# Moving GpSimd's large element-wise products in the front of a hybrid attention/SSM/MoE layer to VectorE and ScalarE

## Chip, cores, metric

The kernel runs on one core of a Trainium2 chip. The metric is the device time of one execution in microseconds (us). The kernel before takes 1189.6 us, the median of 3 runs (1189.0 to 1190.3).

## What is computed

One layer of a streaming encoder, batch 1, 256 frames, 1024 features, fp32, with 16 meta tokens put in front (272 rows). The parts that matter here:

```python
h = layer_norm(concat(meta, x), ln_in_g, ln_in_b)
q, k, v, u = split(h @ w_in)                      # 512 columns each
lam = exp(sum(lq1 * lk1)) - exp(sum(lq2 * lk2)) + lam_init
att = diff_attention(q, k, v, lam, ...)           # 4 heads, two softmaxes each, chunk-causal
ssm = s5_ssm(u, a_re, a_im, log_step, b, c, ...)  # complex diagonal recurrence, then GLU
h = layer_norm(2**0.25 * h + concat(att, ssm) @ w_out, ln1_g, ln1_b)
h = layer_norm(2**0.25 * h + moe(h), ln2_g, ln2_b)  # top 4 of 32 experts, each 3 matrices of 1024x1024
```

## The kernel before, in words

The order of the instructions on each engine is the order of the program text (the schedule is written by hand); every engine works through its own queue in order and waits on semaphores where data is needed. All loads are issued on SyncE's queue (SP), also in order.

**Front** (lines 145 to 870). Rows are loaded, normalised (lines 198 to 217), transposed on TensorE into hT (line 237), and projected with w_in: u first (line 389), then q (439), k and v (`proj`, lines 429 to 434). The SSM is done four frames at a time. VectorE works out the step, the decay and the rotations: `exp_poly` (248) for exponentials, and sines and cosines of 8 multiples of the angle (285 to 309). The table ED (line 314, in buffer slot 6) holds the rotors of 68 steps for 16 blocks; it is filled by doubling, seven steps k of six products or sums each (`cmul`, line 262, called on GpSimd at 324), of 16 times 1, 2, 4, ..., 32 and 4 elements per partition. `powers` (361) multiplies the input matrix Bb by the powers RW (on VectorE, line 381) and the output matrix CC by the powers FW (on GpSimd, line 472); each of its two halves ri is two products of 1024 elements and a sum or difference that is written in two partition halves (line 377 or 375) between zeros into AB. TensorE transposes the input side of AB (459) into BAT, which lies in the buffers that held the temporaries of `cmul` and `powers` (xs5, slots 5a and 5b); ScalarE and VectorE take turns with the copies (463, 465). Then GpSimd overwrites AB with the output side.

**Rounds** (623 to 659). For each of four blocks: `states_a` (TensorE, 553), `states_b` (VectorE, 565 to 577: products, a scan, products), `scores_a` (TensorE 588, VectorE 593, ScalarE's exponentials 597), `scores_b` (VectorE, 602 to 607), with a projection of k or v in between whose copy out of PSUM is ScalarE's. PSUM has 8 banks, handed out in turn by `nb` (77). Meanwhile GpSimd does the output side, a memset (477) and the affine step of the input norm on the residual rows hr (478 to 480).

**Output side of the front** (668 to 868). Products for lags within four frames (674, 678, copied by `lag_b`, 687, into ML), `split_w` (535), which splits w_out into a rounded high part and a low part (cast on ScalarE or VectorE, subtraction on GpSimd or VectorE), `av_a` (726; per head a transpose, copies 735 and 736, and the products 749 of the head before), `av_b`, `out_a` to `out_c`, and `mix` (829) with w_out. Then `norm1` (919), `turn1` (931), `affine1` (937, GpSimd) and the router (`route_a` to `route_c`).

**Experts** (1329 on). 384 chunks of 1 MB of expert weights are streamed through a ring of 18 half-slots (line 488) in the slots 0 to 8; a chunk is issued (`chunk`, 500) when the program has reached it and its half-slot is free. The first chunks are issued between the steps of the front, as its buffers come free: slot 6 after the last `states_b`, slot 3 after w_out's first half is split, slot 4 after `out_a`, the others after the mix and the GLU. One loop at line 1238 handles overfull experts late in the run.

Of the kernel before, what the change touches and what calls it, by code (L numbers as in the profile page):

```python
# [11 lines left out]
F32 = mybir.dt.float32  # L12
# [3 lines left out]
AF = mybir.ActivationFunctionType  # L16
OP = mybir.AluOpType
# [4 lines left out]
D = 1024  # L22
# [42 lines left out]
def hybrid_layer(ctx, tc, I, out):  # L65
# [18 lines left out]
    def slot(i, shape, name, dt=F32):  # L84
        return per.tile(shape, dt, name=name, tag=f"slot{i}")
# [23 lines left out]
    def pt(shape, name, dt=F32, tag=None, bufs=None):  # L109
        return pool.tile(shape, dt, name=name, tag=tag or name, bufs=bufs)  # L110
# [16 lines left out]
    def load(dst, name, off, dims):  # L127
        return SP.dma_start(dst, pap(I[name], off, dims))
# [24 lines left out]
    load_win("u", 0, 1536, 2)  # L153
    for j, n in enumerate(("lambda_q1", "lambda_q2", "lambda_k1", "lambda_k2")):
        load(lam4[:, j, :], n, 0, [[0, 128], [1, 64]])
    eb = slot(6, [128, 4096], "eb")
    bt = eb[:, 3264:3776].rearrange("p (r a c) -> p r a c", r=2, a=16)
    for j, n in enumerate(("b_re", "b_im")):
# [103 lines left out]
    def cmul(eng, dr, di, ar_, ai_, br_, bi_, u, v):  # L262
        eng.tensor_tensor(u, ar_, br_, op=OP.mult)
        eng.tensor_tensor(v, ai_, bi_, op=OP.mult)
        eng.tensor_tensor(dr, u, v, op=OP.subtract)
        eng.tensor_tensor(u, ar_, bi_, op=OP.mult)
        eng.tensor_tensor(v, ai_, br_, op=OP.mult)
        eng.tensor_tensor(di, u, v, op=OP.add)
# [6 lines left out]
            V.tensor_scalar(hT[:, db, :], PS[:, hb[db], :NP], VC[:, db:db + 1], VC[:, 8 + db:9 + db],  # L275
                            op0=OP.mult, op1=OP.add)

    step = pt([128, 16], "step")
    exp_poly(step, LS, 16, "e1")
    sm = [pt([128, 16], f"sm{j}") for j in range(10)]  # L280
    ar, mag, den, er, t1, t2, fr, fi, r4, dt = sm
    V.tensor_scalar(ar, A_RE, -1e-4, None, op0=OP.min)
# [37 lines left out]
    ge = [tq[4 + j].rearrange("p (a c) -> p a c", a=16) for j in range(2)]  # L320
    for k in range(7):
        n = min(2 ** k, 68 - 2 ** k)
        c_, s_ = ((a[:, 1 + k, :, None]).to_broadcast([128, 16, n]) for a in (cs, sn))
        cmul(G, ED[:, 0, :, 2 ** k:2 ** k + n], ED[:, 1, :, 2 ** k:2 ** k + n],
             ED[:, 0, :, 0:n], ED[:, 1, :, 0:n], c_, s_, ge[0][:, :, :n], ge[1][:, :, :n])


    FW = pt([128, 2, 4, 16], "FW")
# [29 lines left out]

    cmul(V, Bb[:, 0], Bb[:, 1], bc16(fr), bc16(fi), bt[:, 0], bt[:, 1], bu, bv)

    def powers(eng, dst, src, tab, sgn, ta, tb):
# [6 lines left out]
        for ri, (j0, j1) in enumerate(((0, 1), (1, 0))):  # L368
            op = sgn[ri]
            eng.tensor_tensor(ta, sv(0), tv(j0), op=OP.mult)  # L370
            eng.tensor_tensor(tb, sv(1), tv(j1), op=OP.mult)
            for g2 in range(2):
                h = slice(64 * g2, 64 * g2 + 64)
                if op == "r":
                    eng.tensor_tensor(dst[h, ri, :, :, g2], tb[h], ta[h], op=OP.subtract)
                else:
                    eng.tensor_tensor(dst[h, ri, :, :, g2], ta[h], tb[h],
                                      op=OP.add if op == "+" else OP.subtract)

    tmp = xs5[0].rearrange("p (r a t c) -> p r a t c", r=2, a=16, t=4)  # L380
    powers(V, AB, Bb, RW, "-+", tmp[:, 0], tmp[:, 1])


    while bank[0] % 4:
# [57 lines left out]
    lt = et([128, 2, 64], "lt")  # L442
    xl, el = et([128, 2], "xl"), et([128, 2], "el")
    V.tensor_tensor(lt, lam4[:, 0:2], lam4[:, 2:4], op=OP.mult)
    V.tensor_reduce(xl, lt, axis=AX.X, op=OP.add)
    exp_poly(el, xl, 2, "e3")
    lam = pt([128, 1], "lam")
    V.tensor_sub(lam, el[:, 0:1], el[:, 1:2])
    V.tensor_scalar(lam, lam, LAM_INIT, None, op0=OP.add)
# [15 lines left out]
                S.activation(BAT[ri][:, 4 * a:4 * a + 4], srcv, AF.Copy)  # L465


    sl0, bc = (slot(f"0{c}", [128, 2, D], "sl0") for c in "ab")
    load(bc[:, 0, :], "ln_in_g", 0, [[0, 128], [1, D]])
    load(bc[:, 1, :], "ln_in_b", 0, [[0, 128], [1, D]])  # L470
    tmc = [sl0[:, j].rearrange("p (a t c) -> p a t c", a=16, t=4) for j in range(2)]
    powers(G, AB, CC, FW, "+r", tmc[0], tmc[1])
    MG = slot(1, [128, 2, 2048], "MG")
    load(MG[:, 1, :], "w_glu", 0, [[512, 128], [128 * 512, 4], [1, 512]])
    ML = MG[:, 0, :].rearrange("p (f q c) -> p f q c", f=4, q=4)
    WG = MG[:, 1, :].rearrange("p (k f) -> p k f", k=4)
# [249 lines left out]
    def av_a(i, between=None):  # L726
        blks = ((0, 128), (1, 16)) if i == 0 else ((0, 128), (1, 128), (2, 16))
        nf = len(blks) - 1
        wts = []
        for h in range(4):  # L730
            tb = nb()
            for blk, n in blks:
                T.transpose(PS[:n, tb, blk * 128:blk * 128 + 128], PW[h, i][:, blk * 128:blk * 128 + n], ident)
            wT = lt_([128, 3, 128], "wT", bufs=2)
            S.activation(wT[:, :nf], PS[:, tb, :nf * 128].rearrange("p (a q) -> p a q", a=nf), AF.Copy)
            V.tensor_copy(wT[:16, nf], PS[:16, tb, nf * 128:nf * 128 + 128])
            wts.append(wT)
# [193 lines left out]
    def turn1(i):
        TB[i] = nb(2)
# [539 lines left out]
```

## Time and profile before

| | |
|---|---|
| median of 3 runs | 1189.6 us |
| the profiled execution's own time | 1188.67 us |
| its span in the profile | 1186.9 us |
| TensorE (PE) busy | 1038.4 us, 87% |
| VectorE (DVE) busy | 360.6 us, 30% |
| ScalarE (ACT) busy | 127.2 us, 11% |
| GpSimd (POOL) busy | 169.6 us, 14% |
| read from HBM | 423.5 MB, 358 GB/s over the span |
| mean granted TensorE clock | 0.952 of full speed |

PE, PEld, DVE, ACT, POOL and SP are TensorE's matmuls and weight loads, VectorE, ScalarE, GpSimd and SyncE. Times in rows are microseconds from the start of the span. L12 is line 12 of the kernel. In `out<-in`, names are the program's tile names; where tiles share memory a row can show another tile's name (xs for the temporaries, sl and s8b for scratch).

### The profile page before, as it was taken

The page shows a single profiled execution, that of the slowest core. Times are in us where ns is not written, and L with a number is a line of the kernel's source. Part 1 is how long each engine was busy: PE and PEld are TensorE (multiplying, and loading weights), DVE is VectorE, ACT ScalarE, POOL GpSimd, SP SyncE. Part 2 cuts the span into 40 slices and gives each one's busy share as a digit, 9 for nine tenths or more (in the row PEclk, how much of TensorE's full clock was granted, in tenths as well). Part 3 has the DMA queues.
Part 4 walks back from the last instruction along what each step waited for, and adds up shares of the span by engine and source line. Part 5 has one row for each costly group of instructions (what it writes and reads, how often), then busy time and mean ns, then how long its engine had stood idle before and what let it go on. Part 6 is the DMA issues. An engine that isn't in the chain of part 4 may idle for free. (4 is left out here: it accounts for less than half of the span.)

```text
span 1186.9 us, 16400 instructions
## 1 busy us (share of the span) xinstructions
PE 1038.4 (87%) x6572; PEld 529.2 (45%) x6572; DVE 360.6 (30%) x737; ACT 127.2 (11%) x286; POOL 169.6 (14%) x259
## 2 busy tenths in 40 slices
PE   6858798989999988999999987899999999998195
PEld 5646686343543443445434433343443344343042
DVE  7999656222212110221122121121122112121113
ACT  1411442100100000001000000000000000000010
POOL 2990414200200110002001011001101010010001
PEclk9978797989999998999999998999999999999699
DMA  7702478789999999999999999999999897999994
GB/s 214 259 0 76 158 270 332 309 324 423 420 421 421 421 420 421 421 420 420 421 421 421 419 421 421 421 421 421 421 412 404 356 403 274 396 365 422 385 372 196
DMA packets 72314, 425.67 MB, mean 359 GB/s; under 512 B 14925, under 2 KB 15546, under 8 KB 23210
## 3 DMA queue, kind: packets, MB, share of 16 engines
q1 hardware_dynamic: 72234, 424.58, 88.5%
q8 instruction: 53, 0.87, 0.3%
q14 instruction: 27, 0.22, 0.1%
HBM read 423.50 MB, written 1.87 MB: 358 GB/s over the span
## 5 line engine op out<-in xcount | busy, mean ns | idle before, releaser
L1156 PE MATMUL PS<-wx,xgp 128*32 128x256 f32 (+2 forms) x3008 | 464.2, 476 | 14.7 <-DMA wx<-in_w_up 8.6
L1156 PEld LDWEIGHTS PS<-wx,xgp 128*32 128x32 f32 (+2 forms) x3008 | 186.5, 130 | 272.8 <-issue 207.8
L1156 PE MATMUL PS<-wx,yT 128*32 128x256 f32 (+2 forms) x1504 | 231.0, 473 | 21.7 <-DVE yT L1189 17.6
L1156 PEld LDWEIGHTS PS<-wx,yT 128*32 128x32 f32 (+2 forms) x1504 | 92.2, 129 | 148.2 <-issue 95.8
L914 POOL COPY si<-P 96x32 bf16<-96x32 bf16 (+2 forms) x32 | 7.4, 234 | 789.3 <-PE PS L1150 759.8
L1178 DVE TENSOR_SCALAR PS<-PS 128x256 f32<-128x256 f32 (+2 forms) x33 | 22.6, 683 | 191.0 <-PE PS L1156 191.0
L1203 DVE COPY yc<-PS 32x256 f32<-32x256 f32 (+1 forms) x39 | 20.1, 514 | 169.0 <-ACT yc L1205 169.0
L1211 PE MATMUL PS<-yc,gt 128*128 128x512 f32 x120 | 58.6, 620 | 13.6 <-DVE yc L1203 5.7
L1212 DVE TENSOR_TENSOR acc<-PS,acc 128x512 f32<-128x512 f32 x60 | 41.4, 691 | 92.9 <-PE PS L1211 92.7
L1150 PE MATMUL PS<-B,si 96*32 96x256 bf16 (+2 forms) x282 | 39.9, 333 | 32.8 <-SPq L1238 25.9
L1118 PEld LDWEIGHTS PS<-ohp,hr 128*128 128x128 f32 x512 | 63.5, 200 | 8.4 <-issue 8.4
L1118 PE MATMUL PS<-ohp,hr 128*128 128x128 f32 x512 | 65.8, 288 | 0.2 <-DVE ohp L1110 0.2
L1172 DVE TENSOR_SCALAR g<-PS 128x256 f32<-128x256 f32 (+1 forms) x27 | 14.9, 553 | 152.5 <-PE PS L1156 122.1
L1205 ACT ACTIVATE yc<-PS 32x256 f32<-32x256 f32 (+1 forms) x39 | 17.4, 446 | 244.2 <-PE PS L1156 237.8
L1211 PEld LDWEIGHTS PS<-yc,gt 128*128 128x128 f32 x120 | 18.7, 188 | 51.6 <-DVE acc L1212 19.8
L1150 PEld LDWEIGHTS <-si 96*32 96x32 bf16 (+2 forms) x282 | 11.8, 100 | 60.0 <-issue 55.2
L1189 DVE COPY yT<-PS 128x512 f32<-128x512 f32 (+1 forms) x39 | 22.5, 590 | 45.2 <-PE PS L1188 45.2
L1173 ACT ACTIVATE PS<-g 128x256 f32<-128x256 f32 (+1 forms) x27 | 13.2, 491 | 206.3 <-DVE g L1172 206.3
L1108 POOL TENSOR_SCALAR gop<-io,PMs,Gs 128x32 f32<-128x32 f32 (+2 forms) x60 | 33.3, 569 | 0.0
L1172 DVE TENSOR_SCALAR yc<-PS 128x1024 f32<-128x1024 f32 x6 | 7.4, 1225 | 78.3 <-PE PS L1156 78.3
L1122 ACT ACTIVATE xgp<-PS 128x512 f32<-128x512 f32 x16 | 9.6, 597 | 192.5 <-PE PS L1118 192.5
L1110 POOL TENSOR_SCALAR ohp<-io,PMs 128x32 f32<-128x32 f32 (+2 forms) x60 | 24.9, 433 | 0.0
(380 smaller groups left out, 847.9 us busy)
## 6 DMA issues: line engine op xcount, KB each, us to landing
wx<-in_w_gate SPq DMA_DIRECT2D x128, 1024.0 KB, 19.7
wx<-in_w_up SPq DMA_DIRECT2D x128, 1024.0 KB, 19.8
wx<-in_w_down SPq DMA_DIRECT2D x127, 1024.0 KB, 19.7
w_u<-in_w_in SPq DMA_DIRECT2D x2, 1024.0 KB
w_q<-in_w_in SPq DMA_DIRECT2D x1, 2048.0 KB
w_k<-in_w_in SPq DMA_DIRECT2D x2, 1024.0 KB
w_v<-in_w_in SPq DMA_DIRECT2D x1, 2048.0 KB
wo<-in_w_out SPq DMA_DIRECT2D x2, 1024.0 KB
```

Source lines behind the costliest of these rows:

```text
L1108: eng.tensor_scalar(dst[:, i, o:o + m], iv, pc, gg[:, i, t:t + 1], op0=OP.is_equal, op1=OP.mult)
L1110: eng.tensor_scalar(dst[:, i, o:o + m], iv, pc, None, op0=OP.is_equal)
L1118: T.matmul(PS[:, 4 + h, k * 128:k * 128 + n], hr[:, i, rows_of(db)], oh_[:, i, :n], start=(i == 0), stop=(i == 1))
L1150: T.matmul(o, sel[:, :m], B96[:, w, f * n:f * n + n], start=True, stop=False)
L1156: T.matmul(PS[(f % nf) * m:(f % nf) * m + m, b + f // nf, :n], xT(kb), c[:, f * n:f * n + n], start=False, stop=(kb == 7))
L1172: V.tensor_scalar(g_, r_, 7.0, None, op0=OP.min)
L1178: V.tensor_scalar(r_, r_, 7.0, -7.0, op0=OP.min, op1=OP.max)
L1189: V.tensor_copy(yT[:, 4 * a:4 * a + nk], PS[:, b, :nk * 128].rearrange("p (k s) -> p k s", k=nk))
L1203: V.tensor_copy(d_, s_)
L1205: S.activation(d_, s_, AF.Copy)
L1211: T.matmul(PS[:, b], gt[:n, i * 128:(i + 1) * 128], yc[:n, h * 512:(h + 1) * 512], start=True, stop=True)
L1212: V.tensor_tensor(acc[:, i, h * 512:(h + 1) * 512], PS[:, b], acc[:, i, h * 512:(h + 1) * 512], op=OP.add)
```

## The change

- `load_win("u")` comes after the four lambda loads; lambda's two sums are made before the transposes are evaluated, and its exponentials share one `exp_poly` with the step.
- The first four rotor steps stay on GpSimd; steps 4 to 6 run on VectorE (`rotors`), after the input side's products.
- `powers` becomes `products` (VectorE, three instructions on all partitions, into a temporary) and `between_zeros` (ScalarE, two copies of 64 partitions into AB). On the input side ScalarE's copies stand between those of the queries, on the output side the whole (`output_matrices`) stands between `scores_a` and `scores_b` of rounds 0 and 1.
- The residual's affine step goes from GpSimd to VectorE, in eight pieces, two after each head's copies in `av_a(0)`. Its two vectors get a slot of their own, 9; the scratch for dynamic DMAs is cut to 1024 bytes to make room.
- `split_w` casts on ScalarE and subtracts on VectorE throughout; the second half of w_out is split in one call, later.
- `norm1(1)` is applied on ScalarE, with a small product (n1) on VectorE in front.

```diff
+    lt = et([128, 2, 64], "lt")
+    V.tensor_tensor(lt, lam4[:, 0:2], lam4[:, 2:4], op=OP.mult)
+    V.tensor_reduce(VC[:, 80:82], lt, axis=AX.X, op=OP.add)
     V.tensor_copy(VC[:, 32:80], PS[:, pb, 304:352])
...
-    step = pt([128, 16], "step")
-    exp_poly(step, LS, 16, "e1")
+    steps = pt([128, 18], "step")
+    exp_poly(steps, VC[:, 64:82], 18, "e1")
+    step, el = steps[:, :16], steps[:, 16:18]
...
-    for k in range(7):
+    def rotors(eng, k, ta, tb):
         n = min(2 ** k, 68 - 2 ** k)
-        cmul(G, ED[:, 0, :, 2 ** k:2 ** k + n], ...)
+        src = ED[:, 0:2, :, 0:n]
+        ta, tb = (t_[:, :32 * n].rearrange("p (j a c) -> p j a c", j=2, a=16) for t_ in (ta, tb))
+        for dst, fac in ((ta, cs), (tb, sn)):
+            for j in range(2):
+                eng.tensor_tensor(dst[:, j], src[:, j], fac[:, 1 + k, :, None].to_broadcast([128, 16, n]), op=OP.mult)
+        new = ED[:, :, :, 2 ** k:2 ** k + n]
+        eng.tensor_tensor(new[:, 0], ta[:, 0], tb[:, 1], op=OP.subtract)
+        eng.tensor_tensor(new[:, 1], tb[:, 0], ta[:, 1], op=OP.add)
+
+    for k in range(4):
+        rotors(G, k, tq[4], tq[5])
...
+    def products(ri, src, tab, op, ta, tb):
...
+        V.tensor_tensor(ta, sv(0), tv(ri), op=OP.mult)
+        V.tensor_tensor(tb, sv(1), tv(1 - ri), op=OP.mult)
+        if op == "r":
+            V.tensor_tensor(ta, tb, ta, op=OP.subtract)
+        else:
+            V.tensor_tensor(ta, ta, tb, op=OP.add if op == "+" else OP.subtract)
+
+    def between_zeros(dst, ri, src):
+        for g2 in range(2):
+            h = slice(64 * g2, 64 * g2 + 64)
+            S.activation(dst[h, ri, :, :, g2], src[h], AF.Copy)
+
+    pwf = lw([128, 1024], "pw", tag="vr")
...
-    powers(V, AB, Bb, RW, "-+", tmp[:, 0], tmp[:, 1])
+    for ri in range(2):
+        products(ri, Bb, RW, "-+"[ri], tmp[:, ri], pw)
+    for k in (4, 5, 6):
+        rotors(V, k, pwf, xs5[1][:, 0:1024])
...
     for h in range(4):
         S.activation(qT[:, h, :], proj("q", h, NM), AF.Copy, scale=0.125)
+        if h % 2:
+            between_zeros(AB, h // 2, tmp[:, h // 2])
...
-    powers(G, AB, CC, FW, "+r", tmc[0], tmc[1])
+    def output_matrices(ri):
+        products(ri, CC, FW, "+r"[ri], tmc[ri], pw)
+        between_zeros(AB, ri, tmc[ri])
...
-    for i in range(2):
-        G.tensor_tensor(hr[:, i], hr[:, i], bc[:, 0], op=OP.mult)
-        G.tensor_tensor(hr[:, i], hr[:, i], bc[:, 1], op=OP.add)
+    def residual_rows(n):
+        for _ in range(n):
+            i, h, j = rr_todo.pop(0)
+            hf = hr[:, i, h * 512:(h + 1) * 512]
+            V.tensor_tensor(hf, hf, bc[:, j, h * 512:(h + 1) * 512], op=(OP.mult, OP.add)[j])
...
-        for k, on_act, eng in ks:
-            if on_act:
-                S.activation(W_HI[j][k], W_OUT[j][k], AF.Copy)
-            else:
-                V.tensor_copy(W_HI[j][k], W_OUT[j][k])
-            eng.tensor_sub(W_LO[j][k], W_OUT[j][k], W_HI[j][k].bitcast(F32))
+        for k in ks:
+            S.activation(W_HI[j][k], W_OUT[j][k], AF.Copy)
+        for k in ks:
+            V.tensor_sub(W_LO[j][k], W_OUT[j][k], W_HI[j][k].bitcast(F32))
...
     scores_a(0, 1)
+    output_matrices(0)
...
     scores_a(1, 1)
+    output_matrices(1)
...
     value_rows(1, vt1)
-    split_w(1, 5, 0, ((0, True, G), (1, True, G)))
...
-    split_w(1, 5, 0, ((2, False, G), (3, False, G)))
+    split_w(1, 5, 0, (0, 1, 2, 3))
...
             wts.append(wT)
+            if i == 0:
+                residual_rows(2)
...
-    split_w(0, 8, 2, ((2, True, G), (0, False, V), (1, True, V)))
+    split_w(0, 8, 2, (0, 1))
     out_a(0)
     out_a(1)
-    av_a(1, lambda: split_w(0, 8, 2, ((3, True, G),)))
+    av_a(1, lambda: split_w(0, 8, 2, (2, 3)))
...
+        if i:
+            n1 = wt([128, 1], "n1")
+            V.scalar_tensor_tensor(n1, m1[:, 0:1], -1.0, r1, op0=OP.mult, op1=OP.mult)
         for f in range(2):
             hf = hr[:, i, f * 512:(f + 1) * 512]
-            V.tensor_scalar(hf, hf, m1[:, 0:1], r1, op0=OP.subtract, op1=OP.mult)
+            if i:
+                S.activation(hf, hf, AF.Identity, bias=n1, scale=r1)
+            else:
+                V.tensor_scalar(hf, hf, m1[:, 0:1], r1, op0=OP.subtract, op1=OP.mult)
```

## Rows read from the trace of the kernel before

**Rows 1.** Windows: us, busy time (x instructions) per engine, granted clock, DMA share, GB/s.

```profile
60.00:80.00 20.00, 13.84 (x64) 11.06 (x64) 18.55 (x12) 1.48 (x3) 19.57 (x10) 0.84 0.00 0
100.00:120.00 20.00, 20.00 (x221) 16.27 (x220) 18.79 (x59) 6.30 (x25) 0.00 (x0) 0.99 0.39 135
...
205.00:210.00 5.00, 4.91 (x24) 3.78 (x26) 4.17 (x16) 0.00 (x0) 2.77 (x1) 0.55 0.00 0
...
300.00:350.00 50.00, 49.10 (x351) 24.43 (x344) 8.26 (x14) 3.62 (x7) 8.32 (x18) 1.00 1.01 420
```

The engine columns of rows 1 are PE, PEld, DVE, ACT and POOL.

**Rows 2.** Waits of SyncE's queue, whole span: us in total, times, longest.

```profile
SPq L522 <- PE PS L1156: 257.6, 138, 18.1
```

**Rows 3.** Timeline, 63 to 87 us, VectorE and GpSimd: start us, us, instruction.

```profile
64.65 5.02 POOL L377 TENSOR_TENSOR AB<-sl 64x1024 f32<-64x1024 f32 x2
64.88 2.58 DVE L568 TENSOR_TENSOR s8b<-s8b 128x272 f32<-128x272 f32 x1
...
84.40 2.34 POOL L480 TENSOR_TENSOR hr<-hr,sl 128x1024 f32<-128x1024 f32 x1
84.44 2.31 DVE L603 TENSOR_TENSOR a<-a,lam 128x1 f32<-128x1 f32 x1
```

**Rows 4.** Timeline, 92 to 127 us, VectorE: the undisturbed rounds and their end.

```profile
92.74 0.71 DVE L565 TENSOR_TENSOR s8b<-PS,eb 128x544 f32<-128x544 f32 x1
...
94.48 0.43 DVE L568 TENSOR_TENSOR s8b<-s8b 128x272 f32<-128x272 f32 x1
...
121.77 4.91 DVE L683 COPY m<-ident 32x32 f32<-32x32 f32 x4
```

**Rows 5.** Timeline, 38 to 64 us, up to the first states_b; idle before in brackets.

```profile
38.11 1.47 DVE L370 TENSOR_TENSOR xs<-xs,RW 128x1024 f32<-128x1024 f32 x1
...
59.31 2.47 DVE L463 COPY BAT<-PS 128x512 f32<-128x512 f32 x4
...
60.40 1.08 ACT L465 ACTIVATE BAT<-PS 128x512 f32<-128x512 f32 x2 [7.32 <-POOL eb L268]
...
63.13 0.72 DVE L565 TENSOR_TENSOR s8b<-PS,eb 128x544 f32<-128x544 f32 x1 [1.35 <-PE PS L553]
```

**Rows 6.** Timeline of VectorE, two-input instructions without GpSimd's products beside them.

```profile
165.23 1.22 DVE L845 TENSOR_TENSOR bf<-bf,bp 96x1024 f32<-96x1024 f32 x1
...
204.76 0.68 DVE L939 TENSOR_TENSOR hr<-hr,bc 128x512 f32<-128x512 f32 x1
```

**Rows 7.** Line 540 on ScalarE, whole span: duration in ns, min/median/max.

```profile
L540 ACT ACTIVATE wh<-wo x5: 1039/1049/1062, 120.8 to 148.6; 128x1024 fp32r<-128x1024 f32 x5
```

**Rows 8.** DMA rate, 0 to 60 us in 40 slices of 1.5 us.

```profile
GB/s 0 134 358 294 367 403 400 233 31 27 64 68 180 367 406 395 291 150 15 63 333 403 404 393 390 384 384 88 72 366 116 30 356 395 249 399 352 5 0 0
```

**Rows 9.** Timeline of VectorE, 127 to 134 us: lag copies, first attention weights.

```profile
127.88 3.16 DVE L696 COPY MG<-KS 32x512 f32<-32x512 f32 x8
...
132.98 0.71 DVE L736 COPY wT<-PS 16x128 f32<-16x128 f32 x2 [0.61 <-ACT wT L735]
```

**Rows 10.** Timeline of VectorE, av_a(1), its copy for head 2.

```profile
150.41 0.28 DVE L736 COPY wT<-PS 16x128 f32<-16x128 f32 x1 [1.42 <-ACT wT L735]
```

**Rows 11.** Windows, from out_a(1) to the mix; columns as in rows 1.

```profile
144.60:161.00 16.40, 16.25 (x134) 14.13 (x133) 8.80 (x16) 7.51 (x20) 3.36 (x2) 1.00 0.37 132
```

**Rows 12.** Timelines of GpSimd and VectorE, 193 to 197 us, norm1(1).

```profile
193.86 1.27 POOL L939 TENSOR_TENSOR hr<-hr,bc 128x512 f32<-128x512 f32 x1
...
193.93 2.88 DVE L929 TENSOR_SCALAR hr<-hr,m,r 128x512 f32<-128x512 f32 x2 [0.67 <-POOL r L195]
```

**Rows 13.** Timeline of TensorE, 94 to 110 us: states_a(2) and states_a(3), projections.

```profile
94.14 3.68 PE L553 MATMUL PS<-u,BAT 128*128 128x68 f32 x16 [10.77 <-DVE s8b L566]
97.61 5.19 PE L432 MATMUL PS<-hT,w_k 128*128 128x272 f32 x16
102.64 3.83 PE L432 MATMUL PS<-hT,w_v 128*128 128x272 f32 x16
...
107.69 1.90 PE L553 MATMUL PS<-u,BAT 128*128 128x68 f32 x16
```

More of the change, by code (lines that the diff above doesn't have):

```diff
@@ L152, in hybrid_layer @@
     load(ls[32:48], "log_step", 0, [[2, 16], [1, 2]])
-    load_win("u", 0, 1536, 2)
     for j, n in enumerate(("lambda_q1", "lambda_q2", "lambda_k1", "lambda_k2")):
         load(lam4[:, j, :], n, 0, [[0, 128], [1, 64]])
+    load_win("u", 0, 1536, 2)
     eb = slot(6, [128, 4096], "eb")
@@ L319, in hybrid_layer @@
     tq = [x_[:, 512 * j:512 * j + 512] for x_ in xs5 for j in range(4)]
-    ge = [tq[4 + j].rearrange("p (a c) -> p a c", a=16) for j in range(2)]
-    for k in range(7):
+    def rotors(eng, k, ta, tb):
         n = min(2 ** k, 68 - 2 ** k)
-        c_, s_ = ((a[:, 1 + k, :, None]).to_broadcast([128, 16, n]) for a in (cs, sn))
-        cmul(G, ED[:, 0, :, 2 ** k:2 ** k + n], ED[:, 1, :, 2 ** k:2 ** k + n],
-             ED[:, 0, :, 0:n], ED[:, 1, :, 0:n], c_, s_, ge[0][:, :, :n], ge[1][:, :, :n])
+        src = ED[:, 0:2, :, 0:n]
[8 more added lines that the diff above has]
+        rotors(G, k, tq[4], tq[5])
     FW = pt([128, 2, 4, 16], "FW")
@@ L359, in hybrid_layer @@
     cmul(V, Bb[:, 0], Bb[:, 1], bc16(fr), bc16(fi), bt[:, 0], bt[:, 1], bu, bv)
-    def powers(eng, dst, src, tab, sgn, ta, tb):
+    def products(ri, src, tab, op, ta, tb):
         def sv(j):
@@ L366, in tv @@
             return tab[:, j].rearrange("p t a -> p a t")[:, :, :, None].to_broadcast([128, 16, 4, 16])
[L368 to L375, printed above, removed]
-                else:
-                    eng.tensor_tensor(dst[h, ri, :, :, g2], ta[h], tb[h],
-                                      op=OP.add if op == "+" else OP.subtract)
+        V.tensor_tensor(ta, sv(0), tv(ri), op=OP.mult)
[9 more added lines that the diff above has]
+    pwf = lw([128, 1024], "pw", tag="vr")
+    pw = pwf.rearrange("p (a t c) -> p a t c", a=16, t=4)
     tmp = xs5[0].rearrange("p (r a t c) -> p r a t c", r=2, a=16, t=4)
-    powers(V, AB, Bb, RW, "-+", tmp[:, 0], tmp[:, 1])
+    for ri in range(2):
+        products(ri, Bb, RW, "-+"[ri], tmp[:, ri], pw)
+    for k in (4, 5, 6):
+        rotors(V, k, pwf, xs5[1][:, 0:1024])
     while bank[0] % 4:
@@ L439, in hybrid_layer @@
         S.activation(qT[:, h, :], proj("q", h, NM), AF.Copy, scale=0.125)
[L442 to L446, printed above, removed]
+        if h % 2:
+            between_zeros(AB, h // 2, tmp[:, h // 2])
     lam = pt([128, 1], "lam")
@@ L465, in hybrid_layer @@
                 S.activation(BAT[ri][:, 4 * a:4 * a + 4], srcv, AF.Copy)
-    sl0, bc = (slot(f"0{c}", [128, 2, D], "sl0") for c in "ab")
+    sl0 = slot("0a", [128, 2, D], "sl0")
+    bc = slot(9, [128, 2, D], "bc")
     load(bc[:, 0, :], "ln_in_g", 0, [[0, 128], [1, D]])
@@ L477, in hybrid_layer @@
     G.memset(MG[:, 0, :], 0.0)
-    for i in range(2):
-        G.tensor_tensor(hr[:, i], hr[:, i], bc[:, 0], op=OP.mult)
-        G.tensor_tensor(hr[:, i], hr[:, i], bc[:, 1], op=OP.add)
+    def residual_rows(n):
[3 more added lines that the diff above has]
+            V.tensor_tensor(hf, hf, bc[:, j, h * 512:(h + 1) * 512], op=(OP.mult, OP.add)[j])
+    rr_todo = [(i, h, j) for i in range(2) for h in range(2) for j in range(2)]
     def rows_of(kb):
@@ L537, in split_w @@
             W_HI[j], W_LO[j] = parts4(s_, "wh", FR), parts4(l_, "wl", FR)
-        for k, on_act, eng in ks:
-            if on_act:
-                S.activation(W_HI[j][k], W_OUT[j][k], AF.Copy)
-            else:
-                V.tensor_copy(W_HI[j][k], W_OUT[j][k])
-            eng.tensor_sub(W_LO[j][k], W_OUT[j][k], W_HI[j][k].bitcast(F32))
+        for k in ks:
+            S.activation(W_HI[j][k], W_OUT[j][k], AF.Copy)
+        for k in ks:
+            V.tensor_sub(W_LO[j][k], W_OUT[j][k], W_HI[j][k].bitcast(F32))
     XS, VB = {}, {}
@@ L607, in scores_b @@
         V.scalar_tensor_tensor(w[:, :nk], s_[:, 0, :nk], r_[:, 0:1], s_[:, 1, :nk], op0=OP.mult, op1=OP.subtract)
-    vr = lw([128, 3, 512], "vr")
     def values(h):
@@ L639, in hybrid_layer @@
     states_b(2)
+    vr = lw([128, 3, 512], "vr")
     vt0 = values(0)
@@ L1461 @@
     from concourse.bass_utils import run_bass_kernel_spmd
-    nc = bacc.Bacc("TRN2", target_bir_lowering=False, num_devices=1)
+    nc = bacc.Bacc("TRN2", target_bir_lowering=False, num_devices=1, dynamic_dma_scratch_size=1024)
     arrays = {f"in_{n}": a for n, a in layout(inputs).items()}
```

## The prediction

> **What bounds the kernel now.** I began with the stages (busy time of each engine by stretch) and asked which of them can pass a saving on. From 300 us on the DMA engines are full at 420 GB/s [rows 1], so the weight stream cannot be made faster there; only its start can move. At 205 to 210 us, just before the first expert, they move nothing [rows 1]: the ring of weight buffers is full, and what was loaded before has slack. From there on a load waits until TensorE releases a buffer: of what SyncE's queue waits for, TensorE's expert products are the longest item, 257.6 us in 138 waits [rows 2]. So the moment at which TensorE starts on the experts sets the stream behind it, and a saving in the front should reach the end nearly one for one.
>
> Inside the front, 60 to 80 us stands out: VectorE and GpSimd are both busy all the time, TensorE only 13.84 of 20 us and DMA not at all; at 100 to 120 us, with GpSimd idle, TensorE is full [rows 1]. The timeline of the two vector engines says why. The subtraction of line 568 takes 2.58 us beside GpSimd's line 377 (two instructions, 5.02 us). A 128x1 product, line 603, takes 2.31 us: it starts 0.04 us after GpSimd's line 480 and ends with it, near 86.75 [rows 3]. The same line 568 takes 0.43 us once GpSimd has stopped [rows 4]. VectorE stands still while GpSimd runs a large product.
>
> **The change part by part.** The sum is made along VectorE's order, against the profiled execution's 1188.67 us.
>
> *1. Up to the first round of states.* Before, states_b(0) starts at 63.13, after ScalarE had waited 7.32 us for GpSimd's rotors, whose temporary its copy overwrites [rows 5]. After, VectorE goes on at 38.11 with six full-height products and sums of 1024 elements. The first of these takes 1.47 us with GpSimd beside it [rows 5]; a 1024-wide two-input instruction without GpSimd takes 1.22, a 512-wide one 0.68 [rows 6]. GpSimd still makes the four small rotor steps for the first few microseconds, so I take three at 1.47 and three at 1.22: 8.1 us, to 46.2. The last three rotor steps are six instructions each, of 256, 512 and 64 elements; the line through the two prices of rows 6 gives 0.41, 0.68 and 0.21: 7.8 us, to 54.0. Then lambda (I take 0.4; its sums and polynomial have moved forward) and four copies of BAT, 2.47 [rows 5]: to 56.9. ScalarE's four writes of halves into AB cost about 1.05 each, the price of a 128x1024 copy there [rows 7]; two fall between the copies of queries and two before the key's, where ScalarE otherwise waits for TensorE's projections: nothing. **-6.2 us.** Bounds: all six at 1.22 gives -7.0; all at 1.47, and VectorE held once by ScalarE's copies for 2.1, gives -3.3.
>
> [...]
>
> The four lambda loads now stand ahead of w_u in SyncE's queue and hold its two issues back by their own four, under 2 us. The traffic that w_u ends is over by the ninth slice of 1.5 us, at 12 [rows 8], and TensorE waits for hT until 14: that wait hides about 2 us; if it doesn't, +1. Lambda's two new VectorE instructions come where VectorE waits for TensorE's transposes: nothing.
>
> *2. The four rounds of states and scores.* Before, 63.13 to 121.77 (where line 683 starts): 58.6 us. The three undisturbed rounds took 92.74 to 121.77, 29.0 us, so 9.7 each [rows 4]. After: four such rounds, 38.7, and output_matrices twice, three instructions at 1.22 each: 7.4. Together 46.1, to 103.0: **-12.5 us.** At 1.47 each it is -11.0. Behind output_matrices scores_b is queued, whose exponentials ScalarE makes meanwhile. ScalarE's four writes of halves (1.05 each) hold back its copies of keys 2 and 3, which are wanted a round later: nothing, or 2 us where TensorE's banks run out.
>
> *3. To the first weights of attention.* Before, 121.77 to 132.98, 11.2 us, of which line 683, four 32x32 copies, takes 4.91 beside GpSimd's subtractions [rows 4, 9]. After, I take 0.7 for it, 0.7 for line 685, 0.3 waiting for KS, 3.16 for line 696 [rows 9]; then four casts on ScalarE at 1.05 [rows 7] and four subtractions on VectorE at 1.22, the first beside the second cast: 4.9 and 1.2 in front. To 114.0, 11.0 us: **-0.2** (-1.5 to +1.5). W_OUT's other loads come earlier with everything else.
>
> *4. The residual's affine step,* four instructions of 2.34 on GpSimd [rows 3], is now eight on VectorE of 512 at 0.68, two after each head's copy in av_a(0), which put 1.4 us between that copy and the next. TensorE's and ScalarE's steps for a head run beside them; at the last head I find VectorE 0.7 us behind. **+0.7** (0 to +2).
>
> *5. split_w(0) in av_a(1).* Two casts (2.1) and two subtractions (2.4) now stand between heads 1 and 2, where one cast stood and the subtraction ran on GpSimd. VectorE's copy for head 2, at 150.41 before [rows 10], comes 1.7 us later. From 144.6 to the mix at 161 TensorE is busy 16.25 of 16.40 us [rows 11], so no gap behind it absorbs that: I take **+1.3** (0 to +2).
>
> *6. norm1(1).* VectorE's two instructions of line 929 take 2.88 us, because GpSimd's line 939 started 0.07 us ahead of them [rows 12]. They go to ScalarE, but the small product n1 ahead of them stays on VectorE and meets the same GpSimd instruction, as line 603 did [rows 3, 12]: it ends near 195.2. ScalarE would then end near 196.5, where VectorE ended at 196.81, but the router's copy of rows 0 is queued behind it on ScalarE, and TensorE's transposes behind the product that wants that copy. **+1.4** (-0.5, if n1 finds a gap, to +1.6).
>
> Sum: -6.2 - 12.5 - 0.2 + 0.7 + 1.3 + 1.4 = -15.5, 1173.2 us for the profiled execution. The median of the runs, 1189.6, lies 0.9 above it: **1174.0**, rounded.
>
> **The rivals.**
> - *The late terms cost nothing* (4 to 6 lie beside other work): -18.9, 1170.7. For it: two of them stand where TensorE waits as well. Against: TensorE full behind term 5 [rows 11]. 0.16.
> - *ScalarE's copies hold VectorE.* If a second product waits until ScalarE has read the first one's half of a temporary, some 2.1 us come back at two or three places: about 1179. Against: the halves are separate. 0.10.
> - *TensorE's clock becomes the bound.* With the clock at its low level a projection took 5.19 us and a set of states 3.68, against 3.83 and 1.90 [rows 13]. Seven projections and four sets would add 16.6 us to the rounds' 43 of TensorE work (an estimate: 20 in two undisturbed rounds [rows 1], and the lag products); the rounds take 60, not 46: 1188, no change. For it: TensorE was idle for 10.77 us ahead of the third set of states [rows 13] and would still wait there. Against: at 100 to 120, with VectorE as tightly packed, the clock was 0.99 [rows 1]. 0.04.
> - *The saving is hidden anyway* in the stream: 1189. Against: DMA idle at 205 [rows 1]. 0.02.
> - *Slower:* VectorE's slow instructions at 63 to 92 us are slow for another reason than GpSimd. The rounds keep 58.6 us and get 7.4 more; with -6.2 in front and +3.2 behind that is +4.4, 1194. Line 568 of the first round decides it: over 2 us with GpSimd idle. Against: line 603 ends with GpSimd's instruction [rows 3]. 0.04.
>
> [...]
>
> **How the numbers follow.** The forecast as summed has 0.64. With every bound on one side the sum runs from -21.5 to -4.2; they will not all fall together, and with the first two rivals taken in, the range is 1167 to 1182. A measurement of this kernel can tell about 0.2%, 2.4 us. Faster: 0.64 + 0.16 + 0.10 = 0.90. The same: 0.04 + 0.02 = 0.06. Slower: 0.04.
>
> **What would show it.** Right: line 568 near 0.43 us in all four rounds; states_b(0) near 57 and scores_b(3) done near 103; each large product near 1.22; the first expert product some 15 us earlier with DMA idle just before it; the rest of the trace the same, only earlier. Wrong: gaps on VectorE ahead of the second products (ScalarE holds it), TensorE busy at a clock of 0.5 between 60 and 100, or a first expert product 15 us earlier without the end following.

## The result and the profile after

The changed kernel takes 1171.52 us, the median of 4 runs (1170.19 to 1172.19); before, beside it, 1189.36. The ratio is 0.9847, 95% interval 0.9832 to 0.9862. Forecast were 1174.0 and a range of 1167 to 1182. The profiled execution took 1170.19 us, its span is 1168.4: both 18.5 less than before. Line numbers have moved: 568 of before is 593, 463 is 479, 683 is 709, 736 is 762, 929 is 957 (n1) and 961.

The page's first part, busy time by engine (us, share, instructions):

```profile
PE 1034.0 (88%) x6572; PEld 527.5 (45%) x6572; DVE 344.5 (29%) x755; ACT 139.5 (12%) x299; POOL 106.9 (9%) x223
```

VectorE took over the products that GpSimd gave up (62.7 us there) and is busy for 16.1 us *less* than before, though it handed only the norm of the last rows (2.88 us) and three casts to ScalarE. Its busy time of before was partly time in which it was held, that is, in which an instruction ran longer than its own price (line 568: 2.58 us for 0.43 [rows 3, 4]).

Windows of the changed kernel, columns as in [rows 1]:

```profile
60.00:80.00 20.00, 16.79 (x91) 13.45 (x90) 19.41 (x49) 6.96 (x20) 0.00 (x0) 0.91 0.09 31
...
186.00:191.00 5.00, 4.71 (x22) 3.90 (x24) 4.20 (x16) 0.00 (x0) 2.77 (x1) 0.50 0.00 2
300.00:350.00 50.00, 47.65 (x270) 23.92 (x270) 10.81 (x15) 4.27 (x9) 5.51 (x14) 1.00 1.01 421
```

GpSimd is silent in the rounds; just before the first expert, now at 190.80, DMA is again idle, and behind it the stream is as full as it was [rows 1]. SyncE's queue still waits longest for TensorE's expert products [rows 2]:

```profile
SPq L549 <- PE PS L1190: 268.9, 140, 20.3
```

The first expert product on TensorE, before and after:

```profile
209.43 3.66 PE L1156 MATMUL PS<-wx,xgp 128*64 128x512 f32 x16
```

```profile
190.80 4.19 PE L1190 MATMUL PS<-wx,xgp 128*64 128x512 f32 x16
```

Timeline of VectorE in the changed kernel (start us, us, instruction, idle before):

```profile
12.47 0.29 DVE L245 TENSOR_TENSOR lt<-lam 128x128 f32<-128x128 f32 x1 [1.08 <-DMA lam<-in_lambda_k]
...
38.94 1.48 DVE L382 TENSOR_TENSOR xs<-xs,RW 128x1024 f32<-128x1024 f32 x1
40.34 1.21 DVE L383 TENSOR_TENSOR pw<-xs,RW 128x1024 f32<-128x1024 f32 x1
...
56.86 0.72 DVE L590 TENSOR_TENSOR s8b<-PS,eb 128x544 f32<-128x544 f32 x1 [0.68 <-PE PS L578]
...
58.61 0.43 DVE L593 TENSOR_TENSOR s8b<-s8b 128x272 f32<-128x272 f32 x1
...
64.00 1.22 DVE L382 TENSOR_TENSOR sl<-s8b,FW 128x1024 f32<-128x1024 f32 x1
...
69.75 0.72 DVE L590 TENSOR_TENSOR s8b<-PS,eb 128x544 f32<-128x544 f32 x1
...
101.98 0.72 DVE L709 COPY m<-ident 32x32 f32<-32x32 f32 x4
...
112.95 0.27 DVE L762 COPY wT<-PS 16x128 f32<-16x128 f32 x1
...
173.68 1.21 DVE L957 SCALAR_TENSOR_TENSOR n<-m,r 128x1 f32<-128x1 f32 x1 [0.67 <-POOL r L195]
```

Line 593 takes 0.43 us in the first round, where it took 2.58 [rows 3]; the four copies of line 709 take 0.72, where they took 4.91 [rows 4]. Two of these rows show VectorE still held: the first product at 38.94, 1.48 for 1.22, and in the last row a 128x1 instruction that takes 1.21 (0.16 in e3 below, with GpSimd idle).

Where each us went, from mark to mark of the two profiled executions:

| from, to | before | after | difference | forecast |
|---|---|---|---|---|
| start to states_b(0) (term 1) | 63.13 | 56.86 | -6.27 | -6.2 |
| to line 683 / 709 (term 2) | 58.64 | 45.12 | -13.52 | -12.5 |
| to the first wT (term 3) | 11.21 | 10.97 | -0.24 | -0.2 |
| to TensorE's out_a(0) (term 4) | 6.44 | 6.02 | -0.42 | +0.7 |
| to the mix (term 5) | 21.55 | 21.89 | +0.34 | +1.3 |
| to the last norm | 30.44 | 30.31 | -0.13 | 0 |
| to the first expert product (term 6) | 18.02 | 19.63 | +1.61 | +1.4 |
| sum: first expert product | 209.43 | 190.80 | -18.63 | -15.5 |

The end moved by 18.5, so the shift passed through the weight stream nearly one for one.

### The profile page after: what moved, and what is told of

Read it like the earlier page. It is cut to its first block, busy times and chain, and to the rows that moved or that the text cites. A ratio compares the mean times of both kernels' runs of the same rounds, so it can differ in the third digit from the quotient of the medians.

```text
span 1168.4 us, 16386 instructions
## 1 busy us (share of the span) xinstructions
PE 1034.0 (88%) x6572; PEld 527.5 (45%) x6572; DVE 344.5 (29%) x755; ACT 139.5 (12%) x299; POOL 106.9 (9%) x223
## 5 line engine op out<-in xcount | busy, mean ns | idle before, releaser
L1152 PEld LDWEIGHTS PS<-ohp,hr 128*128 128x128 f32 x512 | 66.4, 208 | 9.6 <-issue 9.6
L1152 PE MATMUL PS<-ohp,hr 128*128 128x128 f32 x512 | 68.6, 296 | 0.2 <-DVE ohp L1144 0.2
```

The source lines that it names most:

```text
L1152: T.matmul(PS[:, 4 + h, k * 128:k * 128 + n], hr[:, i, rows_of(db)], oh_[:, i, :n], start=(i == 0), stop=(i == 1))
```

## The experiments

All edits are to the changed kernel; line numbers are each kernel's own. The same kernel's runs differ by up to 5 us, so stages are compared mark to mark; where only the medians are compared, against the 1171.52 us above, differences of a few us may be spread, the more so as the runs were made on several chips.

**e0: no edit.**

> The changed kernel as it is, beside the next three on one chip. Theory: 1171.5 us, as first measured; its trace shows the first expert product at 190.8 us, 18.6 earlier than before, and the end 18.5 earlier.

1172.61 us, ratio 0.9855 (0.984 to 0.987). The norm stage (last norm to first expert product) took 18.96 us here, 19.63 above; n1 took 1.21 in both. The difference is mostly TensorE's eight transposes behind it (1.21 us here, 1.95 above). TensorE had waited as long in both, 3.21 us here and 3.20 above, but the mean granted clock behind the wait was 0.87 here (176.30 to 177.70) and 0.50 above (176.66 to 177.66).

**e1: the norm of the last 128 rows back on VectorE.**

```diff
-            if i:
-                S.activation(hf, hf, AF.Identity, bias=n1, scale=r1)
-            else:
-                V.tensor_scalar(hf, hf, m1[:, 0:1], r1, ...)
+            V.tensor_scalar(hf, hf, m1[:, 0:1], r1, ...)
```

> Only norm1(1) goes back to VectorE's two instructions. Theory: in the changed kernel n1 is held by GpSimd's line 973 (1.21 us) and the router's copy and TensorE's transposes then queue behind ScalarE; that edit gave back 1.6 us of the 20.2 that the front had gained by then. Undone: 1.6 us less, 1169.9, with VectorE's two instructions at 2.9 us again. Rival: the edit is neutral and the 1.6 us were lost elsewhere behind the mix: 1171.5.

Measured: 1170.13 us, ratio 0.9832 (0.9819 to 0.9846); norm stage 18.03, as before the change. VectorE and GpSimd in it:

```profile
174.63 1.26 POOL L967 TENSOR_TENSOR hr<-hr,bc 128x512 f32<-128x512 f32 x1
```

```profile
174.70 2.88 DVE L957 TENSOR_SCALAR hr<-hr,m,r 128x512 f32<-128x512 f32 x2 [0.67 <-POOL r L195]
```

The time is as expected (1169.9), though its interval touches e0's. The 2.88 of [rows 12] is back, and still cheaper than the way over ScalarE: by 0.9 us against e0, 1.6 against the changed kernel's first profile.

**e2: e1, and GpSimd's affine step of the first 128 rows behind that of the last. e3: that swap alone.**

```diff
     norm1(1)
-    affine1(0, 1, G)
     route_b(0)
     turn1(1)
     affine1(1, 0, G)
+    affine1(0, 1, G)
```

> norm1(1) back on VectorE, and GpSimd's affine1(0, 1) put behind affine1(1, 0), which waits for TensorE's transposes: so GpSimd stands still while norm1(1) runs. Theory (GpSimd's products hold VectorE): the two instructions take 1.0 us instead of 2.9, TensorE's transposes come 1.9 us earlier than in the run with norm1(1) on VectorE alone: 1168.0. Rival (VectorE is slow there for another reason): as that run, 1169.9.

> The changed kernel with only GpSimd's affine1(0, 1) put behind affine1(1, 0); norm1(1) stays on ScalarE. Theory: n1 takes 0.15 us instead of 1.21, so about 1.0 us less than the changed kernel, 1170.5; what is left of the 1.6 is the order on ScalarE. Rival: n1 was not held by GpSimd: 1171.5.

e2: 1167.57 us, ratio 0.9807 (0.9794 to 0.982); stage 16.78. e3: 1172.41, ratio 0.9847 (0.983 to 0.9863); stage 18.41. VectorE and GpSimd in e2:

```profile
175.37 1.00 DVE L957 TENSOR_SCALAR hr<-hr,m,r 128x512 f32<-128x512 f32 x2 [0.67 <-POOL r L195]
```

```profile
176.70 1.26 POOL L967 TENSOR_TENSOR hr<-hr,bc 128x512 f32<-128x512 f32 x1 [1.37 <-PE PS L962]
```

With nothing of GpSimd beside it the norm takes 1.00 us, not 2.88, and the stage is 1.25 us shorter than e1's, where 1.9 was expected. VectorE and TensorE in e3:

```profile
173.91 0.16 DVE L957 SCALAR_TENSOR_TENSOR n<-m,r 128x1 f32<-128x1 f32 x1 [0.67 <-POOL r L195]
```

```profile
175.83 0.41 PE L995 MATMUL PS<-s,rp 128*128 128x32 f32 x2 [2.16 <-ACT rp L994]
```

In e3 n1 takes 0.16 in place of 1.21, but ScalarE's two halves then take 1.52, more than VectorE's two, and its copy for the router is queued behind them: TensorE waits 2.16 us for that copy. So term 6 has two parts: the hold on n1, which the swap removes, and ScalarE's place in the chain, which only undoing the edit removes. e3's gain in the stage, 0.5 to 1.2 us, doesn't show in its time: 1172.41, not the 1170.5 that was expected.

**e4: the output side's products made twice.**

```diff
-        products(ri, CC, FW, "+r"[ri], tmc[ri], pw)
+        for _ in range(2):
+            products(ri, CC, FW, "+r"[ri], tmc[ri], pw)
```

> The changed kernel, with the six products of output_matrices made twice (same result). Theory: VectorE's order sets the front and all of it reaches the end: six more instructions at 1.22 us, +7.4 us, 1178.9, the first expert product 7.4 us later. Rival (the front is hidden in the weight stream, or TensorE sets the rounds): under +2 us.

1178.87 us, ratio 0.991 (0.9877 to 0.9944): six instructions of 1.22 are 7.3 us, and the median of its two runs is 7.4 over that of the changed kernel. VectorE in e4, at the two ends of the rounds:

```profile
57.59 0.72 DVE L591 TENSOR_TENSOR s8b<-PS,eb 128x544 f32<-128x544 f32 x1 [0.69 <-PE PS L579]
...
110.03 0.72 DVE L710 COPY m<-ident 32x32 f32<-32x32 f32 x4
```

The rounds take 52.44 us, 7.3 more than the 45.12 of the changed kernel. VectorE sets the end of the rounds, and what it takes there arrives at the end undiminished, as far as two runs can tell. (The first expert product came 8.9 us later, at 199.68, not the 7.4 that was expected; the rest lies in stages that the edit does not touch.)

**e5: the six output products on GpSimd. e6: the residual's affine step on GpSimd, ahead of the rounds. e7: rotor steps 4 to 6 on GpSimd.**

```diff
-        products(ri, CC, FW, "+r"[ri], tmc[ri], pw)
+        products(ri, CC, FW, "+r"[ri], tmc[ri], pw, G)
...
-            V.tensor_tensor(hf, hf, bc[:, j, h * 512:(h + 1) * 512], ...)
+            G.tensor_tensor(hr[:, i], hr[:, i], bc[:, j], ...)
...
-        rotors(V, k, pwf, xs5[1][:, 0:1024])
+        rotors(G, k, junk[:, 0:1024], xs5[1][:, 0:1024])
```

> Only the six products of output_matrices go back to GpSimd (about 2.1 us each, 13 us, early in the rounds); ScalarE still writes the halves. Theory: VectorE is spared 7.4 us and held for about 0.7 of GpSimd's 13 us, the share seen before: +2 us, 1173.5, with line 593 over 1.5 us in the first round. Rival (GpSimd does not hold VectorE): -7.4 us, 1164, line 593 at 0.43.

> Only the residual's affine step goes back to GpSimd, in front of the rounds as before (four instructions, 9.4 us). Theory: it holds VectorE for some 0.7 of that, +6 us, 1177.5, and nothing comes back in av_a(0), where VectorE's eight pieces cost nothing. Rival: GpSimd's work beside the rounds is free, 1171.5 or a little less.

> Only the last three rotor steps go back to GpSimd (18 instructions, some 12 us by themselves, beside VectorE's six input products). Theory: each engine holds the other, the rotors end near 57 us and the copy into BAT's second half waits for them: states_b(0) near 59 instead of 56.9, +2 us, 1173.5. Rival (no holding): VectorE is through sooner and states_b(0) comes near 56, -1 us.

e5: 1173.95 us (ratio 0.9869, 0.9822 to 0.9916); e6: 1180.72 (0.9925, 0.9899 to 0.9951); e7: 1176.14 (0.9887, 0.9851 to 0.9923). By the medians the residual on GpSimd costs 9.2 us, the rotors 4.6, the output products 2.4, beside the 17.8 us that the change gained. These are no shares of it that add up: each is one part undone with the others in place. Only the residual's 9.2 is clear of the spread; the intervals of e5 and e7 touch that of the changed kernel, and for them the traces decide. e6 and e7 cost more than was expected of them. GpSimd and VectorE in e5:

```profile
60.40 2.23 POOL L382 TENSOR_TENSOR sl<-s8b,FW 128x1024 f32<-128x1024 f32 x1
```

```profile
60.68 2.26 DVE L593 TENSOR_TENSOR s8b<-s8b 128x272 f32<-128x272 f32 x1
```

Line 593 is held again, as expected, and e5's rounds take 44.89 us, hardly less than 45.12, though VectorE is spared the six products. GpSimd and VectorE in e6:

```profile
52.67 9.51 POOL L510 TENSOR_TENSOR hr<-hr,bc 128x1024 f32<-128x1024 f32 x4
```

```profile
52.55 2.70 DVE L333 TENSOR_TENSOR pw<-eb,cs 128x64 f32<-128x64 f32 x2
55.17 4.67 DVE L333 TENSOR_TENSOR xs<-eb,sn 128x64 f32<-128x64 f32 x2
59.88 2.38 DVE L335 TENSOR_TENSOR eb<-pw,xs 128x64 f32<-128x64 f32 x1
```

These rotor products of 64 elements take 0.35 a pair and 0.23 alone in the changed kernel: GpSimd's four instructions, over 9.5 us, let five small ones of VectorE through, and states_b(0) starts at 65.51, 8.65 later than in the changed kernel. In e7 it is GpSimd's instructions, too, that are held. GpSimd and VectorE in e7:

```profile
43.06 3.16 POOL L333 TENSOR_TENSOR xs<-eb,sn 128x256 f32<-128x256 f32 x2
...
51.65 2.06 POOL L333 TENSOR_TENSOR xs<-eb,sn 128x512 f32<-128x512 f32 x2
```

```profile
45.66 1.64 DVE L383 TENSOR_TENSOR pw<-xs,RW 128x1024 f32<-128x1024 f32 x1
```

Beside VectorE's products a GpSimd product of 256 takes 1.58; one of 512, once they are over, 1.03. VectorE's take up to 1.64 for 1.22. The rotors end at 58 on GpSimd, where VectorE's copies of BAT wait 3.39 us for them, and states_b(0) starts at 60.73, 3.87 later.

**e8: eight GpSimd products on a buffer that nobody uses, ahead of the rounds. e9: ten GpSimd memsets of it instead.**

```diff
+    junk = slot("0b", [128, 2048], "junk")
+    G.memset(junk, 0.0)
+    for _ in range(8):
+        G.tensor_tensor(junk[:, :1024], junk[:, :1024], junk[:, 1024:], op=OP.mult)
```

> The changed kernel, with eight 128x1024 products on GpSimd put in front of the rounds, on a scratch buffer that nobody else uses (about 19 us). No data passes between the engines. Theory (a GpSimd instruction that reads SBUF holds VectorE's instructions with two SBUF inputs): VectorE is held for some 13 us, 1184.5; line 593 over 1.5 us in the first round. Rival (VectorE waited for GpSimd's data or order): 1171.5.

> The same with ten memsets of 128x2048 (about 18 us) in place of the products: GpSimd as busy, but it reads nothing. Theory: VectorE is not held, 1171.5 (up to +0.5), line 593 at 0.43 us. Rival (any GpSimd instruction holds VectorE): +13 us, as with the products.

e8: 1184.88 us (ratio 0.9963, 0.9949 to 0.9978). e9: 1174.37 (0.9869, 0.9851 to 0.9887). GpSimd and VectorE in e8:

```profile
54.69 20.80 POOL L503 TENSOR_TENSOR junk<-junk 128x1024 f32<-128x1024 f32 x8
```

```profile
57.01 0.72 DVE L594 TENSOR_TENSOR s8b<-PS,eb 128x544 f32<-128x544 f32 x1 [0.68 <-PE PS L582]
...
59.70 2.58 DVE L597 TENSOR_TENSOR s8b<-s8b 128x272 f32<-128x272 f32 x1
62.21 5.59 DVE L599 TENSOR_TENSOR_SCAN sw<-eb,s8b 128x272 f32<-128x272 f32 x2
...
75.71 0.43 DVE L606 TENSOR_TENSOR X<-s8b 128x272 f32<-128x272 f32 x1
```

No data passes between the two, and the first round still goes from 12.89 to 26.35 us (29.61 before the change): line 597 takes 2.58 us, what line 568 took before the change [rows 3], and line 606 takes 0.43 as soon as GpSimd is through. Line 594, one of whose two inputs lies in PSUM, keeps its 0.72 beside the same GpSimd products. GpSimd and VectorE in e9:

```profile
54.39 18.60 POOL L503 MEMSET junk<- 128x2048 f32 x10
```

```profile
58.75 0.43 DVE L597 TENSOR_TENSOR s8b<-s8b 128x272 f32<-128x272 f32 x1
...
64.06 1.47 DVE L624 TENSOR_SCALAR a<-a 128x2 f32<-128x2 f32 x1
...
68.06 1.26 DVE L633 TENSOR_SCALAR as<-as,a 128x144 f32<-128x144 f32 x1
```

Beside a GpSimd that only writes, the two-input products and the scans keep their price (one took 1.39 for 1.22); what is held are TENSOR_SCALARs (0.17 and 0.29 without). The first round takes 1.8 us more. By the medians the kernel takes 2.9 more, over the 0.5 that was allowed for, but e9's interval touches that of the changed kernel.

**e10: w_u's loads ahead of lambda's, as before the change; lambda's sums just before the shared polynomial. e11: e2, with the sums in that later place but the loads still in front.**

```diff
-    for j, n in enumerate(("lambda_q1", "lambda_q2", "lambda_k1", "lambda_k2")):
-        load(lam4[:, j, :], n, 0, [[0, 128], [1, 64]])
     load_win("u", 0, 1536, 2)
+    for j, n in enumerate(("lambda_q1", "lambda_q2", "lambda_k1", "lambda_k2")):
+        load(lam4[:, j, :], n, 0, [[0, 128], [1, 64]])
...
+    lt = et([128, 2, 64], "lt")
+    V.tensor_tensor(lt, lam4[:, 0:2], lam4[:, 2:4], op=OP.mult)
+    V.tensor_reduce(VC[:, 80:82], lt, axis=AX.X, op=OP.add)
     steps = pt([128, 18], "step")
```

> The changed kernel with w_u's loads ahead of lambda's again and lambda's two sums right in front of the step's exponential. Theory: in the changed kernel VectorE waited 1.08 us for lambda's load and TensorE started on w_u at 15.2 instead of 14.0; here TensorE starts at 14.0 again, but the sums (0.6 us) now stand in VectorE's row: nothing to -0.5 us, 1171.2. Rival (TensorE's start sets the front): -1.2 us.

> The norm back on VectorE and GpSimd's affine step of rows 0 behind that of rows 1, as in e2, on another chip; besides, lambda's two sums stand behind VectorE's copies of hT, with lambda's loads still in front of w_u. Theory (GpSimd's reads hold VectorE, and the swap takes them away from the norm): the norm on VectorE takes 1.00 us again, from the last norm's start to the first expert product it is 16.8 us (19.6 in the changed kernel, 18.0 with the norm on VectorE alone), and the time is 0.980 to 0.982 of before. The sums: in the run with lambda behind w_u, hT's copies began at 12.74 in place of 13.12, and lambda's wait took 2.09 us because it had landed at 16.80; with the loads in front it has landed by 12.47, so the two sums should wait for nothing and VectorE's first product should start 0.3 to 0.5 us earlier than 38.94. Rival (e2's gain was the spread of its runs): the stage is again near 18 and the time 0.983 to 0.986 of before. Rival on the sums: they only change places, and the first product starts at 38.9 as before.

e10 was a miss: 1177.12 us, ratio 0.9895 (0.9878 to 0.9911), slower by some 5 us. VectorE and TensorE in e10, then TensorE's window in it (columns as in [rows 1]):

```profile
16.80 0.29 DVE L280 TENSOR_TENSOR lt<-lam 128x128 f32<-128x128 f32 x1 [2.09 <-DMA lam<-in_lambda_k]
```

```profile
39.68 12.15 PE L451 MATMUL PS<-hT,w_q 128*128 128x256 f32 x48 [4.68 <-ACT u L413]
```

```profile
40.00:42.00 2.00, 2.00 (x6) 1.55 (x6) 1.97 (x4) 1.98 (x9) 1.70 (x4) 0.50 0.39 144
```

Behind w_u lambda lands at 16.80, and the polynomial that it now shares with the step waits for it: VectorE's first large product starts at 41.39, 2.45 later. ScalarE's copies of u, queued behind an instruction that wants VectorE's result, come late, so TensorE stands still for 4.68 us and comes back at a granted clock of 0.50: 12.15 us for the projections that took 10.63 in the changed kernel (48 matmuls in both), where it had waited 1.72 and kept 1.00. With that states_b(0) starts at 60.84, 4.0 late. Loading lambda first is thus what keeps the shared polynomial from waiting.

e11: 1168.15 us, ratio 0.9827 (0.981 to 0.9843); norm stage 16.78 once more, the norm at 1.00. The late sums gained nothing: they wait for nothing, but the first product starts at 39.21. The 1.08 us in front of them in the changed kernel lay beside TensorE's transposes, for which VectorE waits until 12.53 without them. The ratio is just above what was expected, and just below what the rival gave. e2's gain over the changed kernel, 2.2 to 2.9 us by the stage (18.96 or 19.63 to 16.78), is there on a second chip to the hundredth; in the time e2 lies clear below the changed kernel run beside it (e0), while e11's interval touches those of the changed kernel. e2 is the version that beats both kernels.

## Why the prediction was right, and where it was not

**What bounds the kernel** held: the stream behind the first expert did not change, and e4 shows a price in the rounds arriving at the end in full. **The cause** held: VectorE's slow instructions were slow because of GpSimd's products beside them. e8 makes them slow again with idle products (line 597: 2.58 us), so the slower case (another reason) is out. In e9, beside memsets that only write, the same line takes 0.43: of the two kinds of GpSimd work tried here it was the products, which read SBUF, that held two-input instructions. "VectorE stands still while GpSimd runs a large product" was too wide: in e8 line 594 keeps its 0.72 us.

**Term 1** was right in its sum, by errors that cancel. The first product started at 38.94, not 38.11: the polynomial began 0.35 later (14.99, not 14.64), behind the lambda sums that were costed at nothing, and the rest was lost in the six instructions of 256 elements just ahead of the products, which ran longer beside GpSimd's rotor steps than before (0.51 to 0.62 us each, 0.40 to 0.62 before); and VectorE then waited 0.68 us for TensorE ahead of states_b(0). Against that, only one product met GpSimd, where three were forecast, 0.5 less, and the three rotor steps took 6.95 us (46.44 to 53.39), not 7.8. The price of 1.22 us without GpSimd beside it [rows 6] held for the 1024-wide products of the change: eleven of the twelve took 1.21 to 1.23. The u projection started 1.18 us late (15.18, not 14.00): the wait for hT did not hide the lambda loads as forecast. But nothing followed from that, since ScalarE, which takes u out of PSUM, waited for VectorE until 29.79 in any case.

**Term 2** was 1.0 too small a gain. A round without products takes 9.69 us, as forecast, but one with them 12.88: 3.2 more, not the 3.67 of three instructions at 1.22. The products stand where scores_b would have waited for ScalarE's exponentials anyway (VectorE's next instruction starts behind them without a gap), and back to back they start 1.14 to 1.25 us apart. ScalarE's copies between zeros cost nothing: its row in the changed kernel shows it waiting for VectorE, not the reverse.

```profile
67.65 2.12 ACT L392 ACTIVATE AB<-sl 64x1024 f32<-64x1024 f32 x2 [2.40 <-DVE sl L387]
```

**The rival of TensorE's clock** was half there. After a wait of 3.21 us a set of states took 2.51 us (3.68 and 1.90 in [rows 13]) and the projection behind it 5.09, nearly the slow one's 5.19, but the next projection was at full speed (granted clock 0.79, 0.76 and 1.00 in the three stretches). In [rows 13], too, the slow projection ran only in part at the low level (mean granted clock 0.74 from 97.61 to 102.60; 0.50 over the states ahead of it, 94.14 to 97.61), so the rival's 5.19 is not the price of the low level alone. TensorE's other waits in the rounds were 1.44 us at most, and VectorE, busy for 43.2 of the rounds' 45.1 us, still set the pace. TensorE in the changed kernel:

```profile
71.15 2.51 PE L578 MATMUL PS<-u,BAT 128*128 128x68 f32 x16 [3.21 <-DVE s8b L591]
73.45 5.09 PE L451 MATMUL PS<-hT,w_k 128*128 128x272 f32 x16
78.37 3.83 PE L451 MATMUL PS<-hT,w_v 128*128 128x272 f32 x16
```

**Term 3** was right to 0.04, and by its parts: VectorE waited 1.32 us for ScalarE's casts, where 1.2 was forecast, and its four subtractions took 4.55, not 4.9.

**Term 4**, +0.7, was -0.4: the step that failed is "at the last head I find VectorE 0.7 us behind". It gave TensorE too little time for its steps: in av_a(0) TensorE was at its low level before the change, and it is after; windows of before, then of after:

```profile
133.00:139.40 6.40, 6.40 (x21) 4.47 (x20) 1.09 (x4) 0.83 (x3) 3.87 (x2) 0.50 0.26 72
```

```profile
113.00:119.00 6.00, 5.78 (x20) 4.01 (x19) 5.86 (x13) 0.56 (x2) 0.00 (x0) 0.50 0.17 34
```

A head takes TensorE about 1.76 us there; VectorE needs 1.51 with the residual's two pieces. The cover was wider than the forecast saw, and one window would have shown it. That the term came out below nothing is a matter of the mark, VectorE's first copy: TensorE's first product stood 0.02 us behind that copy before and stands 0.69 ahead of it now. TensorE, before and after:

```profile
133.00 1.52 PE L749 MATMUL PS<-vr,wT 128*128 128x128 f32 x4
```

```profile
112.26 0.80 PE L777 MATMUL PS<-vr,wT 128*128 128x128 f32 x2 [3.17 <-ACT wT L761]
```

Counted from TensorE's first product, term 3 is -0.95 and term 4 +0.29. Their sum, -0.66 where +0.5 was forecast, doesn't depend on the mark.

**Term 5**, +1.3, was +0.3. VectorE's copies for heads 2 and 3 do come late, at 131.23, 1.3 behind out_a(0)'s shift, but TensorE works ahead on the products of the heads before and loses only 0.52 us. The row of TensorE:

```profile
131.56 1.54 PE L777 MATMUL PS<-vr,wT 16*128 16x128 f32 x8 [0.52 <-DVE wT L762]
```

**Term 6**, +1.4, was +1.6, by the mechanism named: n1, on VectorE, meets GpSimd's line 973 (started 0.06 us ahead) and takes 1.21; ScalarE's two halves and the router's copy follow. Its size is in part luck: in e0, the same kernel, the stage was 0.9 longer than before, and most of the other 0.7 here is TensorE's transposes at the low clock (granted 0.50), which the forecast did not have. GpSimd, ScalarE and TensorE of the changed kernel:

```profile
173.62 1.26 POOL L973 TENSOR_TENSOR hr<-hr,bc 128x512 f32<-128x512 f32 x1
```

```profile
174.93 1.52 ACT L961 ACTIVATE hr<-hr,n,r 128x512 f32<-128x512 f32 x2 [1.93 <-DVE n L957]
```

```profile
176.66 0.64 PE L995 MATMUL PS<-s,rp 128*128 128x32 f32 x2 [3.20 <-ACT rp L994]
177.10 1.95 PE L968 MATMUL PS<-ident,hr 128*128 128x128 f32 x8
```

So the time came out between the forecast and the rival "late terms cost nothing": terms 4 and 5 cost nothing or little, term 6 came at its full price here and at two thirds of it in e0. Of the 3.1 us by which the sum to the first expert was short, term 4 is 1.1, term 2 and term 5 are 1.0 each. Against the profiled execution the time was 3.0 below the sum; the median of the runs stood 1.3 above the profiled execution this time, where 0.9 was added.

## What to carry to other kernels

Where VectorE and GpSimd are both full, look for VectorE instructions that end when GpSimd's do: here GpSimd's products held VectorE's instructions with two inputs in SBUF (e8: 2.58 us for 0.43), so moving GpSimd's work to VectorE can shorten VectorE's own busy time (by 16.1 us here). A small instruction at the head of a chain can pay as much for a GpSimd instruction beside it as a large one (n1, 128x1: 1.21 us for 0.16), so reorder GpSimd's queue before moving the chain to a third engine (e2 against the changed kernel). Before costing added VectorE work, read the granted clock of the window that is to hide it.

## What was not expected

- GpSimd's memsets, which read nothing, held VectorE's TENSOR_SCALARs (0.17 to 1.47 us) while its two-input products beside them kept 0.43 and 1.22.
- The hold works both ways: a GpSimd product of 256 took 1.58 us beside VectorE's products, one of 512 without them 1.03.
- After TensorE had waited for 4.68 us its granted clock was 0.50, which cost the projections behind it 1.5 us; after a wait of 1.72 us it was 1.00. After waits of 3.20 and 3.21 us, in two runs of the changed kernel, it was 0.50 just behind the wait in the one (176.66 to 177.66) and 0.87 on average in the other (176.30 to 177.70).
